# Seven of the eighteen input projections of a hybrid layer: plain float32 matmuls on the residual, norm weights scaled into the weights on ScalarE

## The chip, the core and the metric

The kernel runs on one core of one Trainium2 chip. The metric is the device time of one execution in microseconds (us). The kernel before takes 1257.59 us, the median of three runs (1255.88 to 1262.09).

## The reference, cut to what matters

Two layers run over 280 token columns: 16 meta tokens and 256 prompt tokens as one sequence, and 8 decode tokens with states of their own. A layer is a feed-forward half, three mixers side by side, and a second feed-forward half. The width is 1024, everything is float32.

```
def rmsnorm(x, g):
    y = x * rsqrt(mean(x * x) + eps)
    return y * g

h    = x + 0.5 * swiglu(rmsnorm(x, ffn1_norm), ...)
proj = rmsnorm(h, mix_norm) @ w_in              # 1024 -> 18 blocks of 128
u_s5, p_rwkv, x_lru, g_lru = split(proj)        # 3, 11, 2 and 2 blocks
mix  = concat(s5(u_s5), rwkv7(p_rwkv), rglru(x_lru, g_lru)) @ w_out
h    = h + mix
h    = h + 0.5 * swiglu(rmsnorm(h, ffn2_norm), ...)
```

The state-space mixer (s5) is a diagonal complex recurrence with 24 groups of 16 channels; rwkv7 is a matrix-state recurrence; rglru is a gated linear recurrence behind a convolution of width 4.

## The kernel before, in words

**Tiling.** Channels lie on the 128 partitions and the 280 tokens are columns, so the residual `hres` is 8 tiles of 128x280 (one per block k of the 1024 channels). The norm is taken apart: `split_x` (L263) multiplies `hres` by the norm's weights (a column per k) and splits the product into `xh` (rounded to the fp32r type, ScalarE) and `xl` (the rest, VectorE); the factor 1/rms of each token, `rs`, is multiplied in after the matmul.

**A projection in three passes.** `wpiece` (L179) brings a weight in two pieces of 4 k blocks (128x4x128, 256 KB). A piece goes from DRAM into a `stg` buffer by a DMA on SyncE's queue (SP, L188), ScalarE rounds it to `whi` (ACT, L191) and VectorE subtracts to `wlo` (DVE, L192). There are 5 `stg` buffers, shared by all weights of the kernel, the mixers' output projection `w_out` among them; a buffer is free when its last reader is done. `gemm` (L196) then issues three fp32r matmuls for each k: whi x xh (L200), whi x xl (L201), wlo x xh (L202), 24 for a projection of 8 k blocks. `proj(i)` (L1263) does that for block i of `w_in` and leaves it in a PSUM bank of the tag psa.

**Who uses a projection.** In each layer 11 projections feed rwkv7. `do_s` makes the three that feed s5: VectorE evacuates each into `u5` with `rs` multiplied in (L1457, L1461). `s5_restack` (L665) then copies `u5` into `u4`, another arrangement of the channels, with 16 small DMAs on SP (L670); they need all three tiles of `u5`. `s5_group` reads `u4` on TensorE (L681, two chains of four matmuls for each of three groups), `s5_close` reads it again (L719). `do_l` makes the four projections of rglru (`cb`, L1440 and L1442, and `gb`, L1446) and loads the weights of a gate (`gw`, L749).

**Around them.** `rwkv_inverse` (L906 to L1012) inverts small triangular matrices for the chunks of the sequence. For the first batch of chunks it starts on ScalarE (L916 collects the matrices into `AD`), goes through a long chain on VectorE (L926, L928, ..., L947, L949, L954 to L957, transposes L959 and L960), then TensorE (L974), short matmuls (L984, L985), L1000 and L1008. `rwkv_chunks` (L1015 on) begins with transposes through the identity (L175, L177) and follows with L1050, L1091, L1099, L1197 and so on. The products of the mixers go through `w_out` (L1504 on) with the three-pass `gemm`.

**Order.** The program is written in the order of the `do_` calls at L1479 to L1493, but the launch asks Tile's scheduler, which works with a simulated timeline, to set the order of the instructions on each engine (L1600). Within an engine, and within SP's queue, what stands first goes first: an instruction that waits holds back all behind it.

Of the kernel before, what the change touches and what calls it, by code (L numbers as in the profile page):

```python
# [9 lines left out]
F32 = mybir.dt.float32  # L10
F32R = mybir.dt.float32r
I32 = mybir.dt.int32
AF = mybir.ActivationFunctionType
# [4 lines left out]
P = 128  # L18
DM = 1024
KD = 8  # L20
# [4 lines left out]
NT = 280  # L25
# [44 lines left out]
NBW = (5, 5, 4)  # L70
# [4 lines left out]
def tile_hybrid_decode(ctx, tc, *args):  # L75
    nc = tc.nc
    D = dict(zip(_INS + _OUTN, args))
    V, S, G, PE = nc.vector, nc.scalar, nc.gpsimd, nc.tensor
# [3 lines left out]
    wp = ctx.enter_context(tc.tile_pool(name="wp", bufs=3))  # L82
# [9 lines left out]
    def bank(tag):  # L92
        return lambda: ps.tile([P, 512], F32, name=tag, tag=tag, bufs=NPS[tag])

    psA, psB, psC, psD = (bank(t) for t in ('psa', 'psb', 'psc', 'psd'))
    turn = [(psA, psB, psC)[k] for i in range(max(NPS.values())) for k, t in enumerate(('psa', 'psb', 'psc')) if NPS[t] > i]

    def psAB():

        cnt[0] += 1  # L100
        if full[0]:
            return turn[cnt[0] % len(turn)]()
        return psA() if cnt[0] & 1 else psB()
# [75 lines left out]
    def wpiece(src, eng=None):  # L179

        parts = []
        for a in (src if isinstance(src, list) else [src]):
            parts += [a[:, i:min(i + 4, a.shape[1])] for i in range(0, a.shape[1], 4)]
        res = []
        for a in parts:
            kc = a.shape[1]
            st = wp.tile([P, 4, P], F32, name="stg", tag="stg", bufs=NBW[0])
            nc.sync.dma_start(st[:, :kc], a)  # L188
            hi = wp.tile([P, 4, P], F32R, name="whi", tag="whi", bufs=NBW[1])
            lo = wp.tile([P, 4, P], F32R, name="wlo", tag="wlo", bufs=NBW[2])  # L190
            S.activation(hi[:, :kc], st[:, :kc], AF.Copy)  # L191
            (eng or V).tensor_tensor(lo[:, :kc], st[:, :kc], hi[:, :kc].bitcast(F32), op=SUB)  # L192
            res += [(hi[:, i], lo[:, i]) for i in range(kc)]
        return res

    def gemm(out, w, wk, ah, al, ks, first, last):  # L196

        n = len(ks)
        for i, k in enumerate(ks):
            PE.matmul(out, w[wk[i]][0], ah[:, k], start=(first and i == 0), stop=False)  # L200
            PE.matmul(out, w[wk[i]][0], al[:, k], start=False, stop=False)  # L201
            im = PE.matmul(out, w[wk[i]][1], ah[:, k], start=False, stop=(last and i == n - 1))  # L202
        return im
# [37 lines left out]
    def gvec(l, name):  # L241
        o = PV_OFF[name]
        return PV[:, l, o:o + 8]


    hres = actp.tile([P, KD, NT], F32, name="hres")
# [45 lines left out]
    with tc.tile_pool(name="xin", bufs=1) as xin:  # L292
# [10 lines left out]
        for j in range(KD):  # L303
            pt = psAB()
# [359 lines left out]
    def s5_restack(u5, u4):  # L664

        for a in range(4):
            for s in range(4):
                c0, c1 = 8 + NQ * s - (8 if s == 0 else 0), 8 + NQ * s + NQ + (8 if s == 3 else 0)
                o = 0 if s == 0 else 8
                nc.sync.dma_start(u4[32 * s:32 * s + 32, a:NPA:4, o:o + c1 - c0], u5[32 * a:32 * a + 32, :, c0:c1])  # L670
# [74 lines left out]
    def glu_weights(l):  # L745

        gw = [wp.tile([P, 4, P], F32, name="gw", tag="stg", bufs=NBW[0]) for _ in range(3)]
        for k in range(3):
            nc.sync.dma_start(gw[k][:, 0:3], D['s5_glu_w'][l, k * P:k * P + P].rearrange("p (j f) -> p j f", f=P))  # L749
        return gw  # L750
# [494 lines left out]
    def mixers(l, s5, acc, cols, gnext):  # L1245
# [4 lines left out]
        w_in = D['w_in'][l].rearrange("(k p) f -> p k f", p=P)  # L1250
# [7 lines left out]
        def out_tile(nt, tag):  # L1258
            t = s5t.tile([P, nt, 32], F32, name=tag, tag=tag)
            G.memset(t, 0.0)  # L1260
            return t

        def proj(i):  # L1263
            w = wpiece(w_in[:, :, i * P:i * P + P])
            pt = psA()
            gemm(pt[:, :NT], w, ks, xh, xl, ks, True, True)
            return pt

        so = out_tile(12, "sore"), out_tile(12, "soim")
        lw, gu, sh_in, cv_in = (s5[k] for k in ('lw', 'gu', 'sh_in', 'cv_in'))  # L1270

# [163 lines left out]

        def do_l():
            for t in range(2):
                pt = proj(14 + t)
                G.memset(cb[:, t, 0:3], 0.0)
                V.scalar_tensor_tensor(cb[:, t, 3:3 + NPR], pt[:, :NPR], KR, rs[:, :NPR], op0=MUL, op1=MUL)  # L1440
                dv = cb[:, t, 3 + NPR:].rearrange("p (b j) -> p b j", j=4)
                V.scalar_tensor_tensor(dv[:, :, 3], pt[:, NPR:NT], KR, rs[:, NPR:NT], op0=MUL, op1=MUL)  # L1442
                G.tensor_copy(dv[:, :, 0:3], cv_in[:, t, 0:24].rearrange("p (b j) -> p b j", j=3))
            for t in range(2):
                pt = proj(16 + t)
                V.scalar_tensor_tensor(gb[:, t], pt[:, :NT], KR, rs, op0=MUL, op1=MUL)  # L1446
            R['gw'] = glu_weights(l)

# [3 lines left out]
        def do_s():  # L1452
            R['u4'] = R['p2'].tile([P, NPA, NQ + 2 * ND], F32, name="u4", tag="u4")
            G.memset(R['u4'], 0.0)
            for T in range(3):
                pt = proj(T)
                V.scalar_tensor_tensor(u5[:, T, ND:NT].rearrange("p (s c) -> p c s", s=4),  # L1457
                                       pt[:, 0:NPR].rearrange("p (c s) -> p c s", s=4), KR,
                                       rs[:, 0:NPR].rearrange("p (c s) -> p c s", s=4), op0=MUL, op1=MUL)
                for c in (0, NT):  # L1460
                    V.scalar_tensor_tensor(u5[:, T, c:c + ND], pt[:, NPR:NT], KR, rs[:, NPR:NT], op0=MUL, op1=MUL)  # L1461
            s5_restack(u5, R['u4'])
# [18 lines left out]
        do_x()  # L1481
        do_o()
        do_s()
        do_l()
        do_C()
        R['0'] = s5_group(l, R['p2'], s5, u5, R['u4'], 0, so, pc)
# [13 lines left out]
        for kk in ([0, 1, 2, 6, 7], [3, 4, 5]):  # L1500
# [3 lines left out]
            for j in range(KD):  # L1504
                js = slice(j * P, j * P + P)
                w = wpiece([w_out[:, 3:6, js]] if rw else [w_out[:, 0:3, js], w_out[:, 6:8, js]], V if rw else OPE[j % len(OPE)])
                pt = psAB() if rw else psC()
# [38 lines left out]
    for l in range(DEPTH):  # L1546
        last = l + 1 == DEPTH
        acc = ffn(l, 1, acc, ALLC, gvec(l, 'mix_norm'), prev, STATE if l else PREP)
        cols = ALLC if not last else slice(NMETA, NT)
        acc, states_out = mixers(l, s5s[l], acc, cols, gvec(l, 'ffn2_norm'))  # L1550
        prev = states_out
        acc = ffn(l, 2, acc, cols, None if last else gvec(l + 1, 'ffn1_norm'),
                  states_out if last else lambda tp: s5_prepare(l + 1, tp, s5s[l + 1]), STATE if last else PREP)


    with tc.tile_pool(name="fin", bufs=1) as fp:
# [3 lines left out]
        pt = psB()  # L1560
# [10 lines left out]
        for i, (c0, n) in enumerate(groups):  # L1571
            for half in range(2):
                pt = psAB()
# [30 lines left out]
```

## Time and profile before

| | before |
|---|---|
| median of three runs | 1257.59 us |
| the profiled execution | 1260.87 us |
| its span | 1259.2 us |
| mean granted TensorE clock | 0.962 |
| PE busy | 1208.5 us (96%) |
| DVE busy | 974.5 us (77%) |
| ACT busy | 697.9 us (55%) |
| DMA, mean | 149 GB/s |

PE is TensorE, DVE is VectorE, ACT is ScalarE, POOL is GpSimd and SP is SyncE. The span is the profiled part of an execution; 1.67 us of that execution lie around it. Busy shares are means over stages with different limits. In the first layer the seven projections that the change touches run from 286 to 319 us, and the mixers go on to 407 us; the second layer has the same stretch some 621 us later. A granted clock of 1.00 is 2.4 GHz, 0.50 is 1.2 GHz.

### The profile page before, as it was taken

Reading aid. Unit: us, or ns where it says so; the run is one execution under the profiler, and the core shown is the slowest. Engines: PE = TensorE matmul, PEld = TensorE weight load, DVE = VectorE, ACT = ScalarE, POOL = GpSimd, SP = SyncE. Lnnn points to the kernel's source line nnn. Section 1 sums busy time; section 2 is a strip of 40 time slices with the busy share of each in tenths; the row PEclk is TensorE's granted clock in tenths of the full one; section 3 lists DMA queues with packets and bytes.
Section 4 is the critical chain, followed back from the end, with each engine's and each line's share of the span. In section 5 each row is a group of like instructions: output and inputs, shape, how many; then the busy total and the mean of one; then the engine's idle time right before and its main releaser. Section 6 shows DMA issues by size and latency. Waiting matters only on the chain.

```text
span 1259.2 us, 29102 instructions
## 1 busy us (share of the span) xinstructions
PE 1208.5 (96%) x10744; PEld 1151.8 (91%) x10744; DVE 974.5 (77%) x2405; ACT 697.9 (55%) x1529; POOL 161.7 (13%) x325
## 2 busy tenths in 40 slices
PE   7999999999798999999999999999998989999996
PEld 6999999988676999999999999998887779999996
DVE  7899957789577689995777788666877767888764
ACT  4456677564355645667645554556633656555443
POOL 2000000143442300000000000001615330000000
PEclk9999999999776999999999999999996979999999
DMA  7565644533310666564475776654333038777762
GB/s 183 158 187 163 179 145 144 161 99 100 93 29 28 180 179 178 167 176 139 145 212 161 204 198 184 191 168 136 109 88 90 2 91 220 200 202 200 203 181 84
DMA packets 376908, 187.47 MB, mean 149 GB/s; under 512 B 45532, under 2 KB 375352, under 8 KB 376766
## 3 DMA queue, kind: packets, MB, share of 16 engines
q1 hardware_dynamic: 376430, 184.47, 52.8%
q8 instruction: 84, 1.38, 0.5%
q10 hardware_dynamic: 336, 1.15, 0.3%
q14 instruction: 58, 0.48, 0.1%
HBM read 181.31 MB, written 3.37 MB: 147 GB/s over the span
## 4 chain that ended last, share of the span: by engine, by line
PE 86%; DVE 7%; DMA 3%; issue 1%; ACT 1%; POOL 1%; SPq 0%; DVEq 0%; ACTq 0%; POOLq 0%
PE psa L202 11%; PE psa L200 11%; PE psa L201 11%; PE psc L202 7%; PE psc L201 7%; PE psc L200 7%; PE psb L202 6%; PE psb L201 6%; PE psb L200 6%; PE psc L756 1%; PE psc L719 1%; DVE wlo L192 1%; PE psa L177 1%; DMA stg<-in_w_out_dram 1%; PE psc L681 1%
## 5 line engine op out<-in xcount | busy, mean ns | idle before, releaser
L191 ACT ACTIVATE whi<-stg 128x512 fp32r<-128x512 f32 (+2 forms) x664 | 399.3, 609 | 367.4 <-PE psa L201 87.3
L192 DVE TENSOR_TENSOR wlo<-stg,whi 128x512 fp32r<-128x512 f32 (+2 forms) x640 | 426.5, 672 | 129.6 <-ACT whi L191 31.1
L202 PE MATMUL psa<-xh,wlo 128*128 128x280 f32 (+1 forms) x930 | 272.0, 294 | 1.7 <-DVE wlo L192 1.7
L200 PE MATMUL psa<-xh,whi 128*128 128x280 f32 (+1 forms) x930 | 271.5, 293 | 2.0 <-DVE ts L1300 2.0
L201 PE MATMUL psa<-xl,whi 128*128 128x280 f32 (+1 forms) x930 | 271.5, 292 | 0.0
L200 PEld LDWEIGHTS psa<-xh,whi 128*128 128x128 f32 x930 | 175.5, 189 | 4.4 <-DVE ts L1300 2.2
L202 PEld LDWEIGHTS psa<-xh,wlo 128*128 128x128 f32 x930 | 174.8, 188 | 4.6 <-DVE wlo L192 2.3
L201 PEld LDWEIGHTS psa<-xl,whi 128*128 128x128 f32 x930 | 175.4, 189 | 1.6 <-issue 0.7
L202 PE MATMUL psc<-xh,wlo 128*128 128x280 f32 (+1 forms) x498 | 145.6, 292 | 2.1 <-DVE wlo L192 2.1
L201 PE MATMUL psc<-xl,whi 128*128 128x280 f32 (+1 forms) x498 | 145.4, 292 | 0.9 <-DVE xl L265 0.7
L200 PE MATMUL psc<-xh,whi 128*128 128x280 f32 (+1 forms) x498 | 145.6, 293 | 0.7 <-ACT xh L264 0.5
L202 PE MATMUL psb<-xh,wlo 128*128 128x280 f32 (+1 forms) x396 | 114.8, 290 | 0.6 <-DVE wlo L192 0.6
L200 PE MATMUL psb<-xh,whi 128*128 128x280 f32 (+1 forms) x396 | 114.9, 290 | 0.0
L201 PE MATMUL psb<-xl,whi 128*128 128x280 f32 (+1 forms) x396 | 114.8, 290 | 0.0
L202 PEld LDWEIGHTS psc<-xh,wlo 128*128 128x128 f32 x498 | 94.7, 190 | 3.0 <-DVE wlo L192 2.9
L201 PEld LDWEIGHTS psc<-xl,whi 128*128 128x128 f32 x498 | 94.9, 191 | 1.5 <-DVE xl L265 1.0
L200 PEld LDWEIGHTS psc<-xh,whi 128*128 128x128 f32 x498 | 94.8, 191 | 1.2 <-ACT xh L264 0.6
L202 PE MATMUL psb<-hh,wlo 128*128 128x280 f32 (+1 forms) x264 | 76.7, 291 | 0.0
L201 PE MATMUL psb<-hl,whi 128*128 128x280 f32 (+1 forms) x264 | 76.7, 291 | 0.0
L200 PE MATMUL psb<-hh,whi 128*128 128x280 f32 (+1 forms) x264 | 76.7, 290 | 0.0
L202 PE MATMUL psa<-hh,wlo 128*128 128x280 f32 (+1 forms) x264 | 76.5, 290 | 0.1
L201 PE MATMUL psa<-hl,whi 128*128 128x280 f32 (+1 forms) x264 | 76.6, 290 | 0.0
(620 smaller groups left out, 2540.2 us busy)
## 6 DMA issues: line engine op xcount, KB each, us to landing
stg<-in_ffn_w_gate_dram SPq DMA_DIRECT2D x176, 256.0 KB
stg<-in_ffn_w_up_dram SPq DMA_DIRECT2D x176, 256.0 KB
stg<-in_ffn_w_down_dram SPq DMA_DIRECT2D x160, 256.0 KB
stg<-in_w_in_dram SPq DMA_DIRECT2D x72, 256.0 KB
stg<-in_w_out_dram SPq DMA_DIRECT2D x32, 192.0 KB
bc<-ds SPq DMA_DIRECT2D x24, 192.0 KB
stg<-in_ffn_w_down_dram SPq DMA_DIRECT2D x32, 128.0 KB
bc<-ds SPq DMA_DIRECT2D x12, 256.0 KB
```

The source lines that it names most:

```text
L177: PE.matmul(out, a, ident[r, r], start=True, stop=True)
L191: S.activation(hi[:, :kc], st[:, :kc], AF.Copy)
L192: (eng or V).tensor_tensor(lo[:, :kc], st[:, :kc], hi[:, :kc].bitcast(F32), op=SUB)
L200: PE.matmul(out, w[wk[i]][0], ah[:, k], start=(first and i == 0), stop=False)
L201: PE.matmul(out, w[wk[i]][0], al[:, k], start=False, stop=False)
L202: im = PE.matmul(out, w[wk[i]][1], ah[:, k], start=False, stop=(last and i == n - 1))
L681: PE.matmul(px[r][:, a], s5['xbt'][:, 4 * T + a, r], u4[:, 4 * T + a, 8:16 + NQ], start=True, stop=True)
L719: PE.matmul(py[32 * i:32 * i + 32, c0:c0 + n], w, x[:, o:NQ + ND], start=(m == 0), stop=(m == 2), skip_group_check=True, tile_position=(0, ...
L756: PE.matmul(pz[:, :NT], gw[k][:, j], z5[:, k, 0:NT], start=(k == 0), stop=(k == 2))
```

## The change

A second form of projection, `proj32`, is added, and `do_s` and `do_l` call it: 7 of 18 projections in a layer, 14 in the kernel. The 11 of rwkv7, the feed-forward halves and `w_out` keep `gemm`. A `proj32` brings the same two pieces into the same `stg` buffers, by the same queue. ScalarE multiplies each 128x128 block of the piece by the norm's weights of its k (a column of 128 values as the scale), in place, in four instructions. TensorE multiplies it as plain float32 with `hres` itself, one matmul for each k, 8 in a projection. There is no `whi`, no `wlo`, no reading of `xh` and `xl`. The evacuations are as before.

```
+        def proj32(i):
+
+            pt = psA()
+            for a in range(0, KD, 4):
+                st = wp.tile([P, 4, P], F32, name="stg", tag="stg", bufs=NBW[0])
+                nc.sync.dma_start(st, w_in[:, a:a + 4, i * P:i * P + P])
+                for k in range(4):
+                    S.activation(st[:, k], st[:, k], AF.Copy, scale=gvec(l, 'mix_norm')[:, a + k:a + k + 1])
+                for k in range(4):
+                    PE.matmul(pt[:, :NT], st[:, k], hres[:, a + k], start=(a + k == 0), stop=(a + k == KD - 1))
+            return pt
...
         def do_l():
             for t in range(2):
-                pt = proj(14 + t)
+                pt = proj32(14 + t)
...
             for t in range(2):
-                pt = proj(16 + t)
+                pt = proj32(16 + t)
...
             for T in range(3):
-                pt = proj(T)
+                pt = proj32(T)
```

In the changed kernel the DMA of a piece is L1274, the scaling L1276, the matmul L1278, and every line behind them has moved by 12 (the evacuations of `u5` are L1469 and L1473). The scheduler also sets another order. On TensorE, in the first layer, where the first inverse's L974 stands (its first batch, `psb<-AD,EM`), the rows are now these; `stg` is a weight piece, `u_4417` is `u4`, `BK_3517` and `vv` are inputs of the chunk transposes:

```order
L1278 MATMUL psa<-hres,stg 128x280 x15
L974 MATMUL psb<-AD,EM 32x16 x12
L681 MATMUL psc<-u_4417,xbt 128x76 x6
...
L681 MATMUL psc<-u_4417,xbt 128x76 x2
L1000 MATMUL psb<-AD,EM 32x32 x6
L1278 MATMUL psa<-hres,stg 128x280 x2
L681 MATMUL psc<-u_4417,xbt 128x76 x4
L1278 MATMUL psa<-hres,stg 128x280 x2
L681 MATMUL psc<-u_4417,xbt 128x76 x4
```

Behind these rows come the last 8 of the 56 matmuls L1278 and the transposes L175 and L177. Before, all 168 matmuls of the seven projections and then the transposes stood ahead of L974. Now 44 of the 56 stand ahead of it, L681 and L1000 come next, and the last 12 and the transposes follow.

On SP, around the restack of the first layer, the difference reads so (L816 and L827 carry decode values of rwkv7 out to DRAM and back; `gw` is the gate's weights):

```order
+L1274 DMA stg<-in_w_in_dram 128x4x128 x3
+L816 DMA ds<-dT 40x64 x4
+L1274 DMA stg<-in_w_in_dram 128x4x128
+L827 DMA bc<-ds 64x1024 x2
+L1274 DMA stg<-in_w_in_dram 128x4x128 x5
 L670 DMA u_4417<-u_3941 32x3x68
...
 L670 DMA u_4417<-u_3941 32x3x76
+L1274 DMA stg<-in_w_in_dram 128x4x128 x3
 L749 DMA gw<-in_s_glu_w_dram 128x384 x3
```

The last three of the 14 weight pieces now stand behind the 16 DMAs of the restack; before, all stood ahead of it. The seventh piece stands behind L827.

On ACT the same stretch is now in this order (L1416 is a product of rwkv7, L992 and L963 copies of the inverse, L191 the first piece of `w_out`):

```order
L1276 ACTIVATE stg<-stg,pv 128x128 x8
L916 ACTIVATE AD<-EM 32x384 x4
L1416 ACTIVATE bon<-bon,pv 128x280
L1276 ACTIVATE stg<-stg,pv 128x128 x4
...
L963 ACTIVATE TT<-TT 32x16x32 x2
L1276 ACTIVATE stg<-stg,pv 128x128 x5
L992 ACTIVATE TT<-psb 16x3x16
L1276 ACTIVATE stg<-stg,pv 128x128 x8
L992 ACTIVATE TT<-psb 16x3x16
```

The scalings of the sixth and seventh piece stand ahead of L916, where one L191 stood, and those of the last pieces ahead of the copies L992. On VectorE the third evacuation of `u5` (L1469) now stands behind L957 of the inverse, where the one before (L1457) stood ahead of L949 and of L954 to L957.

## Rows read from the trace of the kernel before

**Rows 1.** The page: PE's busy time, its granted clock in tenths, GB/s moved

```profile
PE 1208.5 (96%) x10744; PEld 1151.8 (91%) x10744; DVE 974.5 (77%) x2405; ACT 697.9 (55%) x1529; POOL 161.7 (13%) x325
PEclk9999999999776999999999999999996979999999
GB/s 183 158 187 163 179 145 144 161 99 100 93 29 28 180 179 178 167 176 139 145 212 161 204 198 184 191 168 136 109 88 90 2 91 220 200 202 200 203 181 84
```

**Rows 2.** Stretches: length, busy PE, PEld, DVE, ACT, POOL, clock, DMA, GB/s

```profile
286.00:319.00 33.00, 33.00 (x283) 30.47 (x281) 29.26 (x81) 13.61 (x27) 8.84 (x16) 1.00 0.37 96
319.00:339.00 20.00, 14.85 (x240) 11.70 (x238) 9.69 (x26) 9.05 (x28) 8.28 (x13) 0.82 0.34 95
339.00:360.00 21.00, 19.84 (x454) 17.59 (x452) 14.66 (x31) 5.71 (x18) 10.44 (x20) 0.52 0.30 78
907.00:940.00 33.00, 33.00 (x282) 30.41 (x281) 29.22 (x81) 13.55 (x27) 8.87 (x16) 1.00 0.36 96
```

**Rows 3.** The timeline of PE: start, time, engine, line, operation, out<-in

```profile
304.05 0.29 PE L202 MATMUL psa<-xh,wlo 128*128 128x280 f32 x1
...
306.36 0.29 PE L202 MATMUL psa<-xh,wlo 128*128 128x280 f32 x1
...
319.16 0.28 PE L177 MATMUL psa<-ident,BK 64*16 64x64 f32 x2
...
332.83 0.91 PE L1197 MATMUL psd<-UV,B 128*64 128x64 f32 x12 [2.75 <-ACT UV L1105]
```

**Rows 4.** The chain of waits from 378 us: start, time, what

```profile
379.74 0.47 PE psc L784 x2
```

**Rows 5.** The timeline of PE at half clock, from 396.5 us

```profile
397.15 5.06 PE L756 MATMUL psc<-u,gw 128*128 128x280 f32 x10 [2.43 <-DVE u L731]
```

**Rows 6.** Groups by line and shape, DVE, 286 to 330: busy, mean ns, idle before

```profile
L192 DVE TENSOR_TENSOR wlo<-stg,whi 128x512 fp32r<-128x512 f32 x11 | 7.5, 682 | 0.0
```

**Rows 7.** The same view of ACT, 250 to 300 us

```profile
L191 ACT ACTIVATE whi<-stg 128x512 fp32r<-128x512 f32 x18 | 11.2, 624 | 2.0 <-PE psa L201 1.8
L1302 ACT ACTIVATE ts<-ts,pv 128x272 f32<-128x272 f32 x8 | 4.1, 516 | 6.3 <-DVE ts L1300 6.2
...
L1303 ACT ACTIVATE ts<-stsh_in,pv 128x8 f32<-128x8 f32 x7 | 2.0, 285 | 0.0
```

**Rows 8.** The timeline of DVE around the inverse and the evacuations

```profile
295.57 0.69 DVE L192 TENSOR_TENSOR wlo<-stg,whi 128x512 fp32r<-128x512 f32 x1
...
308.05 0.64 DVE L1457 SCALAR_TENSOR_TENSOR u<-psa,nry 128x272 f32<-128x272 f32 x1
...
310.16 0.68 DVE L192 TENSOR_TENSOR wlo<-stg,whi 128x512 fp32r<-128x512 f32 x1
...
311.64 0.44 DVE L957 TENSOR_SCALAR wk<-XI,hm 128x256 f32<-128x256 f32 x1
```

**Rows 9.** The timeline of SP's queue

```profile
289.57 1.49 SPq L827 DMA_DIRECT2D bc<-ds  x2
...
308.76 11.38 SPq L670 DMA_DIRECT2D u<-u  x16
...
321.82 6.26 SPq L188 DMA_DIRECT2D stg<-in_w_out_dram  x4
```

**Rows 10.** The timeline of ACT

```profile
291.93 2.12 ACT L916 ACTIVATE AD<-EM 32x384 f32<-32x384 f32 x4 [0.57 <-DVE EM L904]
...
325.41 0.83 ACT L191 ACTIVATE whi<-stg 128x384 fp32r<-128x384 f32 x2 [2.05 <-DMA stg<-in_w_out_dram]
```

**Rows 11.** The chain of waits, 284 to 345 us

```profile
327.03 4.46 DMA stg<-in_w_out_dram
```

**Rows 12.** Groups by line, PE, 319 to 339 us: busy, mean ns, idle before

```profile
L681 PE MATMUL psc<-u,xbt 128*128 128x76 f32 x32 | 4.1, 277 | 0.0
...
L985 PE MATMUL psb<-TT,Zs 32*16 32x16 f32 x24 | 0.9, 174 | 0.0
...
L984 PE MATMUL psb<-Zs,TT 32*32 32x16 f32 x12 | 0.8, 186 | 0.0
```

## The prediction

> **What bounds the kernel now.** I read the page first. PE is busy for 1208.5 us, and its granted clock falls below full in two places only [rows 1]: these are in the mixers' stretches, one in each layer. Then I cut the first layer's mixers into stretches [rows 2]. From 286 to 319 us, where the seven projections run, PE is busy for 33.00 of 33 us at clock 1.00, DVE for 29.26, ACT for 13.61. The second layer reads the same, 33.00 of 33 from 907 to 940. So in this stretch PE decides and DVE is close behind; what PE gets more of here, it pays. From 319 to 339 PE is busy for 14.85 of 20 us, and from 339 to 360 for 19.84 of 21 at clock 0.52: here PE waits first and is slow afterwards. The reader should see two regimes: a full one, in which the change replaces matmuls, and a waiting one behind it, into which the changed order moves some of them.
>
> **PE's work.** From 304.05 to 306.36 there are 18 steps of fp32r matmuls [rows 3], so one takes 2.31 / 18 = 0.128 us and the three of a k block 0.385. A plain float32 matmul with 280 columns shows as a pair of records, and one behind another takes 0.47 us at full clock [rows 4]. The changed k block is thus dearer by 0.085 us. There are 56 in a layer: +4.8 us, and +9.5 us for both layers. With PE full up to 319, this is on the path unless it moves to where PE waits.
>
> The Trainium skill (FP8 and Floating Point Precision, section TensorE Precision Notes) says that true FP32 takes four passes through the array. By its four passes against three, at 0.128 us each, a k block would be dearer by 0.128 us and the layer by 7.2; the row of 0.47 us is lower than 0.51, and I go by the row.
>
> **DVE's and ACT's work.** L192 takes 682 ns [rows 6], and 14 of them go in a layer: 9.5 us less on DVE. On ACT 14 of L191 at 624 ns go (8.7 us) and 56 scalings of 128x128 come. The rows hold no such instruction; the nearest have the same kind of scale operand, 516 ns for 272 columns and 285 ns for 8 [rows 7]. On the line between them 128 columns take 0.39 us, so 21.8 us come: +13.1 us in a layer on ACT. ACT has 19 of 33 us idle in that stretch, which hides the sum, but not every place: ACT goes in order.
>
> **Start of the restack.** L916, which starts the first inverse, ran at 291.93 [rows 10]. Now eight scalings stand ahead of it, and the seventh piece is issued behind L827, which ends at 291.06 [rows 9]. How long a piece takes to land with the queue free isn't shown. Bounds: 262 kB at the 200 GB/s of the page's busy slices [rows 1] need 1.3 us; the first `w_out` piece, with three loads ahead of it, is read at 325.41, 3.6 us after its issue at 321.82 [rows 9, 10]. I take 2.5, the middle. Then come four scalings: 291.06 + 2.5 + 1.6 = 295.1, so L916 is 3.2 us late (nothing at the least, 5.8 with the late landing and eight scalings behind it). The VectorE chain behind it loses five L192, the first at 295.57 and the last at 310.16 [rows 8], which gives back 3.4 us. L957 was done at 312.08 [rows 8]. Without the evacuation that stood ahead of it (0.64 us) it is done at 312.08 + 3.2 - 3.4 - 0.6 = 311.3. The third evacuation of `u5` now comes behind it, 0.8 us with its small parts, so the restack starts at 312.1 where it started at 308.76 [rows 9]: +3.3 us. The least is +2.0, from the 24 k blocks of the three s5 projections at 0.085; the most +5.9.
>
> **The last three pieces.** They are now issued behind the restack, whose 16 DMAs hold SP for 11.38 us [rows 9]: 312.1 + 11.4 = 323.5. The first lands 2.5 us later at 326.0, the third two times 1.3 us behind it at 328.6. Its four scalings (1.6 us) and four matmuls (1.9 us) end the projections at 332.1. Before, the transposes behind the projections began at 319.16 [rows 3]: they now begin 12.9 us later. This is the wait that the change adds. Queued behind the waiting matmuls on PE are the transposes, and behind these all of the chunks' recurrence; on ACT the copies L992 and the first `w_out` piece wait behind the scalings; on SP `gw` and `w_out` stand behind the pieces.
>
> **What fills the wait.** L974, L681, L984, L985 and L1000 now stand ahead of the late matmuls. L681, L984 and L985 took 4.1 + 0.8 + 0.9 us between 319 and 339 [rows 12], the others somewhat under 1: 6.6 us in all. PE's 14.85 us of that stretch [rows 2] lose these and the 0.3 us of the last projection: 8.0 are left. 332.1 + 8.0 = 340.1 against 339.0: +1.1 us, if nothing stalls. One stall stays, I think: PE waited 2.75 us for ACT at 332.83 [rows 3], when ACT sat behind `w_out` pieces whose DMA stands in the chain of waits with 4.46 us [rows 11]. The `w_out` pieces are issued no earlier now and ACT still holds their copies among those of the recurrence. +1.1 + 2.75 = +3.9 us in a layer. DVE's saving beyond the five counted, 6.1 us, I cost at nothing: behind 319 it has idle time (9.69 busy of 20).
>
> **The sum.** Two layers: +7.8 us. Against the profiled execution, 1260.87 (a span of 1259.2 and 1.67 around it), that is 1268.7. This execution lies 3.3 us above the median, so I expect a median of 1257.6 + 7.8, about 1265.
>
> **Rivals.**
> 1. No change. The late matmuls fill what was idle, and ACT's stall behind `w_out` goes because the chunk work now starts later than those pieces land. Then +1.1 us in a layer remain, 1257.6 + 2.2 = 1260. For it: 5.15 us of PE were idle between 319 and 339 [rows 2]. Against it: the `w_out` pieces are late by the same three pieces.
> 2. Faster. With the least of each bound (restack +2.0, landing 1.3 us) the projections end at 308.76 + 2.0 + 11.4 + 1.3 + 2.6 + 3.5 = 329.6, and the same 8.0 us lead to 337.6: -1.4 us in a layer. On top, the stretch from 339 to 360 ran at clock 0.52 behind the waits of PE at 332.83 and later [rows 2, 3]. If those waits are gone, the clock stays up there and 19.84 us of PE work shrink towards 10; DVE's 14.66 us [rows 2] then bound the stretch, so at most 6.3 us come back. Half of that with the -1.4 is -4.6 in a layer: 1248. Against it: the changed order has a wait of its own, so a low clock is moved rather than removed.
> 3. Slower by far. PE waits for the restack between L974 and the late pieces, the clock falls to half, and the 12 late matmuls run at it. The row at half clock has ten records, five matmuls, in 5.06 us, 1.01 each [rows 5]: 12 x 0.54 = 6.5 us on top of 3.9, so 10.4 in a layer and 1278. It decides from the point at which the clock is at 1.2 GHz before the late matmuls begin. For it: after 331 us the clock did fall behind waits of 1 to 3 us, and the wait I work out between 319 and 326 is longer than the work in it.
>
> The Trainium skill (TensorE: Matmul & The Clock Gate, section "HAM oscillation") speaks for the third: a matmul stream that waits on DMA again and again drops to the low clock and pays for it after each gap. By that rule the late matmuls, which wait on three DMAs in a row, would run at 1.2 GHz, and the third rival's 1278 would be the time; the trace's clock of 0.52 behind the waits agrees with the rule.
>
> **How the numbers follow.** My forecast, a median near 1265 with 3 to 4 us either way, has 0.32; the first rival 0.20, the second 0.25, the third 0.23. The bound between a change and none is 0.5%, 6.3 us, about what a measurement of this kernel can tell: 1251.3 and 1263.9. Slower then has the third rival and 0.23 of the forecast, together 0.46; within the bound are the first rival and the forecast's lower end, 0.29; faster is the second, 0.25. The range: below, the second rival's 1248 nearly whole, so 1249; above, 1278 and the latest restack (+2.6 us more in a layer) would be 1283, of which I leave out the end: 1281. The forecast's own range is 1261 to 1269.
>
> **What would show it.** Right: two records per L1278 with 0.47 us for the pair; PE full up to the first inverse's L974; the restack some 3 us later in the stretch; an idle PE before the late L1278 with DMA `stg` or ACT as releaser; L175 and L177 starting some 13 us later; `w_in` pieces issued behind L670 on SP. Wrong in sign: the granted clock between 339 and 360 at 1.00, the recurrence ahead of its old place at 360, and the second layer's mixers shorter than before. Wrong in size: L1278 slower than 0.47 us at full clock (the weights of plain float32 not hidden), L1276 far from 0.39 us, or L916 on time. The prediction fails altogether if the mixers' later stretches (360 to 407), which I left as they are, change by more than these terms.

## The result, and the profile after

The changed kernel takes 1272.08 us (median of four runs, 1269.59 to 1275.31); the kernel before took 1256.78 us in the four runs beside it. The ratio is 1.0101, with a 95% interval of 1.0071 to 1.0131: about 12.7 us slower (8.9 to 16.5 by the interval). The two medians lie 15.3 us apart; the text goes by the ratio, which has an interval. The profiled execution took 1271.79 us (span 1269.8).

The stretches of the changed kernel, with the same columns as [rows 2]:

```profile
286.00:319.00 33.00, 30.97 (x222) 23.53 (x220) 20.49 (x61) 13.24 (x35) 6.48 (x13) 1.00 0.28 75
319.00:339.00 20.00, 17.68 (x186) 13.41 (x186) 9.69 (x28) 7.53 (x25) 7.24 (x15) 0.83 0.34 98
339.00:360.00 21.00, 17.19 (x508) 14.25 (x509) 15.33 (x31) 8.50 (x26) 10.78 (x19) 0.90 0.30 79
```

VectorE's busy time (the third busy field) fell from 29.26 to 20.49 us in the projections' stretch: the relief is there. PE is no longer full in it (30.97 of 33). And from 339 to 360 the granted clock is 0.90 where it was 0.52. The mean clock of the whole span rose from 0.962 to 0.973 in a kernel that became slower, so the mean clock alone does not tell the time.

Where the time went, by two marks in each layer: the norm's first matmul ahead of the mixers (L278) and the last addition to the residual behind them (L1509 before, L1521 after). First the kernel before, on PE and DVE:

```profile
239.37 0.64 PE L278 MATMUL psd<-ones,acc 128*128 128x1 f32 x6
431.87 0.44 DVE L1509 TENSOR_TENSOR hres<-psc,hres 128x280 f32<-128x280 f32 x1
860.33 0.64 PE L278 MATMUL psd<-ones,acc 128*128 128x1 f32 x6
1048.34 0.43 DVE L1509 TENSOR_TENSOR hres<-psc,hres 128x264 f32<-128x264 f32 x1
```

Then the changed kernel:

```profile
238.04 0.64 PE L278 MATMUL psd<-ones,acc 128*128 128x1 f32 x6
433.58 0.44 DVE L1521 TENSOR_TENSOR hres<-psc,hres 128x280 f32<-128x280 f32 x1
861.04 0.64 PE L278 MATMUL psd<-ones,acc 128*128 128x1 f32 x6
1056.55 0.43 DVE L1521 TENSOR_TENSOR hres<-psc,hres 128x264 f32<-128x264 f32 x1
```

The first layer's mixers go from 431.87 - 239.37 = 192.5 us to 195.5, the second's from 188.0 to 195.5: +3.0 and +7.5, together 10.5. The spans differ by 10.6 us, so nothing is left for the rest of the kernel. The loss is in the mixers, as was to be expected. It is not equal in the two layers because the layers were not equal before. The changed kernel's first layer is 1.3 us early when its mixers begin (238.04 against 239.37); the comparisons below add that.

SP's queue of the changed kernel, first layer:

```profile
310.05 10.46 SPq L670 DMA_DIRECT2D u<-u  x16
320.61 1.64 SPq L1274 DMA_DIRECT2D stg<-in_w_in_dram  x3
322.34 7.51 SPq L749 DMA_DIRECT2D gw<-in_s_glu_w_dram  x3
333.07 2.26 SPq L188 DMA_DIRECT2D stg<-in_w_out_dram  x2
```

Against [rows 9] the restack starts 310.05 + 1.3 - 308.76 = 2.6 us later in the layer. The three late pieces follow at 320.61, and `w_out` is issued at 333.07 where it was issued at 321.82: `gw` and `w_out` take buffers of the same five `stg` buffers, which the late pieces hold. PE there:

```profile
309.36 7.34 PE L1278 MATMUL psa<-hres,stg 128*128 128x280 f32 x30
316.63 0.38 PE L974 MATMUL psb<-AD,EM 16*32 16x16 f32 x24
...
319.46 1.09 PE L681 MATMUL psc<-u,xbt 128*128 128x76 f32 x8 [1.85 <-DMA u<-u]
321.91 1.11 PE L681 MATMUL psc<-u,xbt 128*128 128x76 f32 x4 [0.90 <-DMA u<-u]
...
324.45 2.23 PE L1278 MATMUL psa<-hres,stg 128*128 128x280 f32 x4 [0.96 <-ACT stg L1276]
...
331.82 3.10 PE L1278 MATMUL psa<-hres,stg 128*128 128x280 f32 x12
334.85 0.22 PE L175 MATMUL psa<-ident,vv 64*16 64x64 f32 x1
...
337.12 0.38 PE L1008 MATMUL psb<-TT,Z 32*32 32x32 f32 x12
```

L974 is early (316.63), and then PE waits three times, for the restack's DMAs and for the scaling of the first late piece. Two of the late matmuls run at half clock (four records in 2.23 us; the granted clock from 324 to 328 us is 0.50), the last six at full clock (twelve in 3.10). The transposes begin in earnest at 334.85 where they began at 319.16 [rows 3]. The chain of waits names the cause (start, time, what):

```profile
320.61 3.30 DMA stg<-in_w_in_dram
...
323.99 0.41 ACT stg L1276
...
324.45 2.23 PE psa L1278 x4
```

The late piece's load is itself on the path of this layer's mixers, where before no `w_in` load was.

On ACT the scalings and the first copies read:

```profile
293.83 2.12 ACT L916 ACTIVATE AD<-EM 32x384 f32<-32x384 f32 x4
...
323.99 1.28 ACT L1276 ACTIVATE stg<-stg,pv 128x128 f32<-128x128 f32 x4 [11.23 <-DMA stg<-in_w_in_dram]
...
335.50 0.52 ACT L191 ACTIVATE whi<-stg 128x384 fp32r<-128x384 f32 x1 [7.13 <-DMA stg<-in_w_out_dram]
```

L916 is 293.83 + 1.3 - 291.93 = 3.2 us late [rows 10]. ACT stood idle for 11.23 us for the late piece and 7.13 us for the first `w_out` piece.

### The profile page after: what moved, and what is told of

Read it like the earlier page. It is cut to its first block, busy times and chain, and to the rows that moved or that the text cites. A ratio compares the mean times of both kernels' runs of the same rounds, so it can differ in the third digit from the quotient of the medians.

```text
span 1269.8 us, 28919 instructions
## 1 busy us (share of the span) xinstructions
PE 1214.5 (96%) x10632; PEld 1143.5 (90%) x10632; DVE 958.4 (75%) x2377; ACT 712.8 (56%) x1613; POOL 151.7 (12%) x325
## 4 chain that ended last, share of the span: by engine, by line
PE 76%; DVE 12%; DMA 6%; ACT 3%; issue 2%; SPq 1%; DVEq 0%; ACTq 0%
PE psa L202 10%; PE psa L200 9%; PE psa L201 9%; PE psc L201 6%; PE psc L202 6%; PE psc L200 6%; PE psb L202 6%; PE psb L201 6%; PE psb L200 6%; DMA stg<-in_ffn_w_gate_dram 2%; PE psa L1278 2%; DVE wlo L192 1%; PE psc L719 1%; DMA bc<-ds 1%; PE psa L177 1%
## 5 line engine op out<-in xcount | busy, mean ns | idle before, releaser
L191 ACT ACTIVATE whi<-stg 128x512 fp32r<-128x512 f32 (+1 forms) x636 | 382.4, 608 | 355.7 <-PE psa L201 68.1
L192 DVE TENSOR_TENSOR wlo<-stg,whi 128x512 fp32r<-128x512 f32 (+1 forms) x612 | 406.5, 671 | 127.6 <-ACT whi L191 36.0
L200 PE MATMUL psa<-xh,whi 128*128 128x280 f32 (+1 forms) x818 | 238.3, 292 | 2.6 <-DVE ts L1312 2.0
L202 PE MATMUL psa<-xh,wlo 128*128 128x280 f32 (+1 forms) x818 | 238.1, 293 | 2.2 <-DVE wlo L192 2.2
L201 PE MATMUL psa<-xl,whi 128*128 128x280 f32 (+1 forms) x818 | 237.9, 291 | 0.0
L200 PEld LDWEIGHTS psa<-xh,whi 128*128 128x128 f32 x818 | 154.2, 189 | 4.8 <-DVE ts L1312 2.2
L202 PEld LDWEIGHTS psa<-xh,wlo 128*128 128x128 f32 x818 | 153.6, 188 | 4.8 <-DVE wlo L192 3.0
L201 PEld LDWEIGHTS psa<-xl,whi 128*128 128x128 f32 x818 | 154.0, 188 | 1.1 <-issue 0.7
```

## The experiments

Theory A: the loss comes from the late pieces, that is, the three weight pieces queued behind the restack. Rivals: B, the plain matmuls' own time; C, the scalings on ScalarE; D, anything else that the new projections bring, so that the order alone would cost nothing. Each kernel was compared with the kernel before on the same chip; ratios are to it, with 95% intervals.

| kernel | late pieces | plain matmuls in a layer | ratio | interval |
|---|---|---|---|---|
| the change | 3 | 56 | 1.0101 | 1.0071 to 1.0131 |
| e1_s_only | 0 | 24 | 1.0042 | 1.0013 to 1.0071 |
| e2_l_only | 3 | 32 | 1.0274 | 1.0216 to 1.0332 |
| e4_noscale | 3 | 56 | 1.0079 | 1.0053 to 1.0105 |
| e5_restack_pool | 0 | 56 | 1.0052 | 1.0021 to 1.0083 |
| e6_pe_equal | 3 | 46 | 1.0101 | 1.0073 to 1.0130 |
| e9_both | 0 | 46 | 1.0089 | 1.0057 to 1.0121 |
| b5_pool_before | 0 | 0 | 1.0118 | 1.0093 to 1.0142 |
| e7_restack_last | between | 56 | 1.0137 | 1.0106 to 1.0168 |
| b11_late_before | 3 | 0 | 1.0052 | 1.0033 to 1.0071 |
| e10_pieces_first | 0 | 56 | 1.0023 | 1.0003 to 1.0044 |
| e12_first_equal | 0 | 46 | 1.0004 | 0.9985 to 1.0023 |
| e13_dve_scale | 0 | 56 | 1.0136 | 1.0110 to 1.0162 |

**Half of the change each.**

```
e1:  do_l calls proj as before
e2:  do_s calls proj as before
```

> Only the three s5 projections of a layer use the new form; the four of rglru stay on three fp32r passes. In the order of this kernel all weight pieces stand ahead of the restack on SP. Theory A (the loss comes from the last weight pieces being queued behind the restack, so that PE waits for DMA, drops to half clock and starts the chunk recurrence late): with no late pieces most of the loss goes, 1257 to 1262 us. Theory B (the loss is the plain float32 matmuls' own time, 0.085 us a k block, wherever they stand): 24 of 56 k blocks, 24/56 of +15, so 1263 us. Theory C (ScalarE's 56 scalings delay the inverse and the restack): 24 of 56 scalings and these ahead of the inverse's start, 1264 us.

> Only the four rglru projections of a layer use the new form; the three of s5 stay as before. The order of this kernel still has three weight pieces behind the restack on SP. Theory A: most of the loss stays, 1266 to 1272 us, though only 32 of 56 k blocks are changed. Theory B: 32/56 of +15, 1265 us. Theory C: the inverse starts on time, 1259 us.

With the s5 projections alone the loss is 0.4%; the interval, 1.6 to 8.9 us, reaches into what each of the three theories expected. With the rglru projections alone it is 2.7%, far beyond every theory, and more than the whole change. So the halves of this change do not add up. The projections' stretch of e2 shows why it can't be used to weigh A:

```profile
286.00:319.00 33.00, 32.12 (x201) 27.86 (x202) 23.73 (x68) 14.72 (x42) 8.20 (x15) 0.75 0.24 65
```

Its clock is 0.75 in the projections themselves, where it was 1.00 [rows 2]: from 308 to 320 us it is 0.50 while PE is busy all the time. Why it fell there was not traced. Its restack started at 319.76 only.

**No scaling.**

```
-                for k in range(4):
-                    S.activation(st[:, k], st[:, k], AF.Copy, scale=...)
```

> The changed kernel without the 56 scalings of a layer: the norm's weights are left out of the seven projections, all else and the order on SP (three pieces behind the restack) as in the changed kernel. Theory A: 1268 to 1272 us (1.3 us of scaling goes from the wait of the last pieces in each layer). Theory B: 1271 us. Theory C: 1258 to 1263 us.

Measured 1.0079: C falls as the cause of the whole. Some 2.8 us (0.0101 - 0.0079) may belong to the scalings, but the two intervals overlap.

**The plain matmuls' own time.**

```
+                n = KD - 1 - (i % 2)
+                for k in range(min(4, n - a)):
                     PE.matmul(..., stop=(a + k == n - 1))
```

> The changed kernel with 10 of the 56 plain float32 matmuls of a layer left out (the last k block of an even projection, the last two of an odd one, so the sums are incomplete): 46 x 0.47 = 21.6 us of matmul time in a layer, as much as the 168 fp32r matmuls had (168 x 0.128). Three weight pieces still stand behind the restack on SP. Theory B (the loss is the plain matmuls' own time): no difference from the kernel before, ratio 0.998 to 1.002. Theory A (the loss is the wait of the late pieces): ratio 1.006 to 1.010. Both together, each with its half: 1.003 to 1.006.

The ratio is the change's own, 1.0101, with PE given back the 4.7 us of 10 matmuls in each layer. B falls as the whole cause: with the late pieces there, a kernel with less PE work is no faster by any difference that these intervals, 0.3% either way, could show. SP and PE of this kernel:

```profile
307.05 10.91 SPq L670 DMA_DIRECT2D u<-u  x16
318.06 1.63 SPq L1274 DMA_DIRECT2D stg<-in_w_in_dram  x3
```

```profile
319.38 2.38 PE L681 MATMUL psc<-u,xbt 128*128 128x76 f32 x10 [1.50 <-DMA u<-u]
322.13 1.30 PE L1279 MATMUL psa<-hres,stg 128*128 128x280 f32 x2
...
327.02 4.32 PE L1279 MATMUL psa<-hres,stg 128*128 128x280 f32 x12
```

The restack started 3 us earlier than in the change, but the first three late matmuls took 1.30 us each and the last six 0.72 each (4.32 / 6), where the last six of the change took 0.52.

**The restack from another queue.**

```
-                nc.sync.dma_start(u4[...], u5[...])
+                nc.gpsimd.dma_start(u4[...], u5[...])
```

> The changed kernel with the 16 DMAs of the restack issued from GpSimd's queue instead of SP's; in its order all 14 weight pieces stand ahead of gw and w_out on SP and wait for no restack. Theory A: the wait of PE between L974 and the late matmuls shrinks, 1258 to 1264 us. Theory B: 1270 to 1273 us. Theory C: 1269 to 1273 us.

> The same 10 matmuls left out, and the restack issued from GpSimd's queue, so that no weight piece stands behind it. If the plain matmuls' own time and the late pieces are together the whole loss, and GpSimd issues the restack at no cost, this is as fast as the kernel before or a little faster for VectorE's saving: ratio 0.994 to 1.001. If GpSimd's issue has a price of its own, 1.002 to 1.006.

> The kernel before with its restack issued from GpSimd's queue; nothing else changed. It says what that queue is worth without the new projections. Theory A: in the kernel before no weight piece waits for the restack, so little is gained: ratio 0.997 to 1.002. If the queue itself frees gw and w_out and so the chunk work: 0.990 to 0.996. If GpSimd is dear: above 1.003.

On the change this took the ratio to 1.0052, as A expected (6.5 us more than before, where A said at most 7). But the control settles nothing in A's favour: on the kernel before the same edit costs 1.18%. And e9, with less PE work than e5, came out at 1.0089, above both of the ranges that were expected of it, though its interval overlaps that of e5. Moving the restack to GpSimd has a price that depends on the order around it; GpSimd's queue is held by it,

```profile
309.77 8.85 POOL L670 DMA_DIRECT2D u<-u  x16 [4.98 <-DVE wlo L192]
```

(b5), and why that costs 15 us in one kernel and less than nothing in the other was not traced. A needed a test that changes the order on SP and no engine.

**The restack called later.**

```
-            s5_restack(u5, R['u4'])      # in do_s
+        s5_restack(u5, R['u4'])          # behind do_l()
```

> The changed kernel with the restack's call placed behind the four rglru projections in the program; on SP the three late pieces now stand between the restack's DMAs, and on PE all 56 plain matmuls stand ahead of L974. Theory A: the pieces are issued earlier, PE does not wait for them, ratio 1.002 to 1.007 (its remainder the plain matmuls' time and a restack that ends a little later). Theory B: 1.008 to 1.012, as the changed kernel.

1.0137, not faster than the change: a miss for A as I had put it. The scheduler placed the three pieces, and then the three `gw` loads, between the restack's DMAs, so the restack, which took 10.46 us in the change, ran from 312.83 to 327.05:

```profile
312.83 1.44 SPq L670 DMA_DIRECT2D u<-u  x2
314.38 0.53 SPq L1274 DMA_DIRECT2D stg<-in_w_in_dram  x1
...
325.82 1.23 SPq L670 DMA_DIRECT2D u<-u  x2
```

It exchanged one late transfer for another, and doesn't tell A from the rest. On PE all 56 matmuls run through without a wait, to 325.4 us, so the wait for late pieces is not what makes this kernel slow.

**Order on SP, both ways.** An edge of order ties the pieces and the restack on SP, and no instruction is changed (in e10 the restack's call also moves into `do_l`). The scheduler then orders PE anew as well: in b11 L974 and part of L681 stand ahead of the last matmuls of the projections, as in the change, and in e10 all 56 and the transposes stand ahead of L974, as in the kernel before. So these runs test the late pieces together with the order on PE that goes with them. In b11 the kernel before gets the change's order; in e10 the change gets the order of the kernel before:

```
b11 (before):  the DMAs of the last three pieces
+    with tc.issue_after(<last DMA of the restack>): nc.sync.dma_start(st, ...)
e10 (change):
+    with tc.issue_after(<DMA of the last piece>): s5_restack(u5, R['u4'])   # in do_l, no more in do_s
e12:  e10, and the 10 matmuls of e6 left out
```

> The kernel before, with only the order on SP changed: the last three of the 14 weight pieces of the s5 and rglru projections of a layer are issued behind the 16 DMAs of the restack, as in the changed kernel. No plain float32, no scaling. Theory A (the late pieces are the loss): PE waits some 5 us for the pieces, falls to half clock, and the chunk work starts late; ratio 1.006 to 1.012. Theory D (the loss needs the new projections, by their own time, the scaling or the evacuation that moved behind the inverse): ratio 0.998 to 1.004.

> The changed kernel with the opposite order on SP: all 14 pieces of a layer are issued, then the restack. On PE all 56 plain matmuls and the chunk transposes then stand ahead of L974, as in the kernel before. The restack starts when the last piece has a buffer, by my count near 313.5 us in the first layer (310.05 in the changed kernel). Theory A: PE no longer waits for the pieces; what is left is the plain matmuls' own time, now all on the path (at most 4.6 us in a layer), and the later restack: ratio 1.003 to 1.008. Theory D: as the changed kernel, 1.009 to 1.012.

> The same order (all pieces, then the restack), and 10 of the 56 plain matmuls of a layer left out, so that their time equals that of the 168 fp32r matmuls before (the sums are incomplete). With the wait and the own time both gone theory A expects the time of the kernel before, ratio 0.997 to 1.003, so that the difference to the kernel with all 56 is the own time where nothing hides it, 0.004 to 0.007. Theory D, by the scaling or by the evacuation that moved: 1.006 and more.

b11: 1.0052, an interval of 1.0033 to 1.0071. The late order costs 4 to 9 us in a kernel without a single plain matmul. The ratio lies between the two ranges, below A's 1.006 and above D's 1.004, and the interval touches both: the order alone has a price, about half of the change's loss. Its SP queue, and the stretch behind the projections:

```profile
310.91 11.60 SPq L675 DMA_DIRECT2D u<-u  x16
322.61 1.63 SPq L193 DMA_DIRECT2D stg<-in_w_in_dram  x3
```

```profile
319.00:339.00 20.00, 15.81 (x99) 14.01 (x100) 11.54 (x29) 4.41 (x10) 8.92 (x15) 0.57 0.37 107
```

The clock there is 0.57 (0.82 in [rows 2]), and the last matmul of the projections starts at 338.06 us instead of 319.

e10: 1.0023, 1.0003 to 1.0044; the change's interval begins at 1.0071. Of the 12.7 us only some 3 are left, a little less than A expected and far from D. In its queue the pieces come first, and PE runs through:

```profile
300.72 12.86 SPq L1274 DMA_DIRECT2D stg<-in_w_in_dram  x5
313.67 10.42 SPq L670 DMA_DIRECT2D u<-u  x16
...
325.76 7.77 SPq L188 DMA_DIRECT2D stg<-in_w_out_dram  x4
```

```profile
309.61 13.00 PE L1278 MATMUL psa<-hres,stg 128*128 128x280 f32 x54
325.07 0.38 PE L974 MATMUL psb<-AD,EM 16*32 16x16 f32 x24
```

The third evacuation stands behind L957 in e10 too, and the 56 scalings are there, so neither is enough for the main loss (L957 is at 309.27, the evacuation, L1471 there, at 309.61). The restack starts at 313.67, as I had counted, 3.6 us later than in the change, and `w_out` is issued at 325.76 instead of 333.07: here a later restack costs less than late weights. e12 is the kernel before to within its interval (1.0004), so the plain matmuls' own time is the likely remainder of e10; the intervals of the two overlap, so its size, about 0.2%, is not shown.

**A way on that failed.** As e10, with the weights' scaling as one VectorE instruction a piece:

```
-    S.activation(st[:, k], st[:, k], AF.Copy, scale=...)        # 4 of them
+    V.tensor_tensor(st, st, <norm's 4 columns, broadcast>, op=MUL)
```

> The kernel with all pieces ahead of the restack, with the norm's weights multiplied in by one VectorE instruction a piece (128x512, a broadcast operand) instead of four on ScalarE. If the scalings on ScalarE ahead of L916 are part of what is left (the first inverse starts some 2 us later in the changed kernel than before), the ratio to the kernel before falls from 1.002 to between 0.996 and 1.001. If VectorE's chain of the inverse pays as much for the 14 multiplications of 0.68 us as the kernel before paid for L192, it stays at 1.001 to 1.005.

Slower by 1.4%, above both ranges. The multiplications stand in VectorE's order ahead of the first inverse and wait there for the pieces' loads:

```profile
L1275 DVE TENSOR_TENSOR stg<-stg,pv 128x512 f32<-128x512 f32 x14 | 10.9, 779 | 5.3 <-DMA stg<-in_w_in_dram 5.3
```

The inverse's chain starts (L926) at 303.60 and its L957 runs at 317.75, where [rows 8] had 311.64; the restack starts at 316.85. No version was found that beats the kernel before.

## Why the prediction was right, and where it was short

The forecast was 1265 us, +7.8; measured were 1272.08 and +12.7. That is within the whole range (1249 to 1281) but above the forecast's own 1261 to 1269, between it and the third rival's 1278. The direction, the place and the cause of the wait (the late pieces) were right. The size of the wait was not, and the working of what follows it was not: its errors had opposite signs, and that the first layer's +3.9 came close to the measured +3.0 is luck.

- PE's work: a plain pair was to take 0.47 us; 30 records in 7.34 us make 0.49 a pair. So the extra 4.8 us in a layer are there. On the path they cost little that the runs can show: e6, with PE's work made equal, has the change's ratio, and e12 and e10 differ by 0.2% within overlapping intervals.
- ACT's work: 0.39 us for a scaling, from two rows; L1276 takes 389 ns:

```profile
L1276 ACT ACTIVATE stg<-stg,pv 128x128 f32<-128x128 f32 x36 | 11.6, 389 | 21.2 <-DMA stg<-in_w_in_dram 21.1
```

- Start of the restack: L916 3.2 us late as worked out (3.2), the restack 2.6 us late against 3.3. The third evacuation stands behind L957, as the order said:

```profile
309.02 0.42 DVE L957 TENSOR_SCALAR wk<-XI,hm 128x256 f32<-128x256 f32 x1
309.37 0.61 DVE L1469 SCALAR_TENSOR_TENSOR u<-psa,nry 128x272 f32<-128x272 f32 x1
```

- The last three pieces: this is the term that was mis-sized. I had the projections end 12.9 us later than before; by the rows of PE it is 334.92 + 1.3 - 319.16 = 17.1. The restack started 0.7 us earlier than I had it and held SP 0.8 us less, but three parts were left out: the first piece landed 3.3 us after its issue where I took 2.5; I counted only the third piece's four matmuls behind the loads, though sixteen records of L681 stand among the late ones (1.83 + 1.01 us from the same timeline); and two late matmuls ran at half clock. These parts make 3.4 us of the 4.2 by which the projections ended later than I had them.
- What fills the wait: this step failed. L974, L984, L985, L1000 and half of L681 did fill the wait. But the 2.75 us that PE waited for ACT at L1197 [rows 3], which I kept in the sum, are gone in both layers, although ACT's idle time ahead of the first `w_out` copy grew from 2.05 to 7.13 us:

```profile
346.83 0.57 PE L1197 MATMUL psd<-UV,B 128*64 128x64 f32 x12
```

- The later stretches: L1197 is 346.83 + 1.3 - 332.83 = 15.3 us late, and L756 still 397.01 + 1.3 - 386.65 = 11.7, where the sum had 3.9 left at 339 us and nothing after it. Then L756 gives most of it back. Before, it stretched from 386.65 to 402.2 at half clock; these rows come ahead of the one in [rows 5]:

```profile
386.65 2.23 PE L756 MATMUL psc<-u,gw 128*128 128x280 f32 x4
...
390.56 2.23 PE L756 MATMUL psc<-u,gw 128*128 128x280 f32 x4 [1.42 <-ACT tf L722]
```

Now it takes 6.5 us from 397.01:

```profile
397.01 2.15 PE L756 MATMUL psc<-u,gw 128*128 128x280 f32 x8
400.54 3.00 PE L756 MATMUL psc<-u,gw 128*128 128x280 f32 x10 [1.37 <-DVE u L731]
```

Its 18 records take 5.15 us instead of 9.52, and the waits and the work between them shrink too. At its end the layer is 2.7 us late. The second layer gives back as much there, from 15.0 us late at the start of L756 to 6.5 at its end; it was later when it got there. The prediction had said that it fails altogether if the stretches from 360 to 407 change by more than its terms. They changed by 9 us, so by its own sign the working behind 339 us does not hold, though the total does.
- The rivals: the first's condition came (PE's stall for ACT went), but it rested on projections that end 12.9 us late, and they ended 17.1 late. The second's condition came in the main, clock 0.90 from 339 to 360, and yet the kernel was slower: the work had moved behind the wait. The third came in part: the clock fell in the wait, and two matmuls of twelve ran wholly at half clock. The Trainium skill's rule that a matmul stream that waits on DMA again and again drops to the low clock (TensorE: Matmul & The Clock Gate, section "HAM oscillation") agrees with these rows, and with b11's 0.57 from 319 to 339, in direction; as the prediction read it, all twelve would have run at 1.2 GHz, and the rows show the last six at 2.4.

Not settled: b11 (1.0052) has the late order and e6 (1.0101) has it too, with PE work of the same length, and they differ by 0.5%; their intervals just miss each other. The scalings, the evacuation behind L957 or the scheduler's other order are left for that; e4 puts the scalings at about 0.2%, within overlapping intervals, and e12 (1.0004) keeps scalings and evacuation.

A rival that no run isolates is the granted clock behind the projections, which another order of instructions changes as well. Between the two marks, in the one traced execution of each kernel, the mixers read:

| kernel | first layer, us | clock | second layer, us | clock |
|---|---|---|---|---|
| before | 192.5 | 0.88 | 188.0 | 0.89 |
| the change | 195.5 | 0.93 | 195.5 | 0.91 |
| b11_late_before | 199.7 | 0.88 | 188.8 | 0.91 |
| e10_pieces_first | 190.2 | 0.92 | 194.0 | 0.86 |
| e12_first_equal | 188.7 | 0.91 | 191.9 | 0.90 |
| b5_pool_before | 200.5 | 0.85 | 191.2 | 0.90 |
| e7_restack_last | 202.6 | 0.83 | 198.7 | 0.87 |
| e2_l_only | 206.7 | 0.85 | 216.0 | 0.81 |

The results that no theory covers (e2, e7, b5's first layer) have clocks of 0.81 to 0.87 there, below the 0.88 and 0.89 of the kernel before. And the order's price is not the same in both layers: b11 lost nearly all in the first, and e10 took back 5.3 us of the change in the first and 1.5 in the second, where its clock was 0.86 against 0.91. So the ratios show that the order on SP, with the order on PE that follows it, makes most of the loss; how that divides into waiting and clock is open.

## What to carry to other kernels

Before counting an instruction's own time, look at what the change does to the order of the queue that feeds it: here the weight loads that slid behind a run of small dependent transfers cost more than the dearer matmuls did, and one edge of order in the program took most of the loss back. Where several streams share a pool of buffers and one queue, a late user holds back all that follow, so charge a late load with everything behind it. And with a scheduler in between, half an edit is not half its price: compare orders before comparing times. A total that comes out near the forecast says little about its terms: check each of them, and both layers, against the rows.

## What was not expected of the hardware

A higher mean clock went with a longer time (0.973 and 1271.79 us against 0.962 and 1260.87). In the first layer the clock rose from 0.52 to 0.90 between 339 and 360 us, and L756 ran at full clock instead of half, but the chunk work began some 17 us later. And issuing the restack's 16 DMAs from GpSimd instead of SP cost the kernel before 1.18% (1.0093 to 1.0142), though the run of the 16 issues was shorter there, 8.85 us against 11.38 [rows 9].
